# A hybrid streaming-encoder layer: a 32-byte filler in SBUF, later loads of x rows, and a bound on the run ahead at each group's end

## The chip, the cores and the metric

The kernel runs on one core of a Trainium2 chip. The metric is the device time of one execution in microseconds (us), lower is better. The time before is the median of three runs. One further execution was profiled; its trace is what the views of this document are taken from.

## What is computed

One layer on x (256 tokens of 2048 features, float32) and memory (256 tokens), in float32. The reference, cut to what matters here:

```python
h = rms_norm(x, ffn1_norm)
x = x + 0.5 * swiglu_ffn(h, ffn1_w_in, ffn1_w_out)      # 2048 -> 2 x 5632 -> 2048
h = rms_norm(x, mix_norm)
p = h @ w_mix_in                                        # 2048 -> 4096
a_val, a_gate, g_u, g_v = jnp.split(p, split_at, axis=-1)
ya = conv_module_group(a_val, a_gate, ...)              # GLU, causal conv 31, LayerNorm, swish
yb = spatial_gating_group(gelu(g_u), gelu(g_v), ...)    # 8 masked 128x128 mixes
x = x + concat(rms_norm(ya), rms_norm(yb)) @ w_mix_out
h = rms_norm(x, xattn_norm)
x = x + memory_cross_attention(h, rms_norm(mem, mem_norm), w_q, w_kv, w_o)   # 4 heads of 512
h = rms_norm(x, ffn2_norm)
x = x + 0.5 * swiglu_ffn(h, ffn2_w_in, ffn2_w_out)
return rms_norm(x, final_norm)

def swiglu_ffn(h, w_in, w_out):
    gate, up = jnp.split(h @ w_in, 2, axis=-1)
    return (silu(gate) * up) @ w_out
```

Where `rms_norm(x, g)` is x divided by the root of its mean square over the features, times g.

## The kernel before

**Products in two halves.** Every float32 operand is held as a high part (rounded to the matmul's type, "fp32r") and a low part (the rest), and a product is three matmuls: high by high, high by low, low by high. A weight of 128 x 1024 arrives by DMA in a raw place (`raw`, `spare`, `raws_out`), ScalarE (ACT) casts it to the high part (line 451 in the feed-forwards, 128 elsewhere), VectorE (DVE) subtracts to get the low part (lines 428 and 129), and TensorE (PE) uses it as the moving operand, 512 columns at a time, with a 128 x 128 block of x (`x_hl`) or of the hidden layer (`hA`, `hB`, `hC`, `hl_s`) as the stationary one.

**The two feed-forwards** (class `FeedForward`) are the stages the change touches. Each has 11 groups of 512 gate and 512 up columns (`w_in`), then two blocks of 1024 output columns (`w_out`). Group 0 (`begin`) takes 16 weights one after the other, each used by 12 matmuls (`by_two`, lines 358 to 361). Each later group (`group`) takes 8 pairs of weights, some by a scheme with seven products in place of eight (`seven`: four items, of 6, 6, 6 and 3 matmuls, lines 345 to 347), the others plainly (`plain`: two items of 12). Three plain weights of most groups are "summed": their low part is made by two passes of ACT (lines 566, 567) and a DMA that adds, into `hl_s` or `more`, and they need no place of their own. At a group's end its eight PSUM banks are joined by DVE (`joins_eights`, line 702), and `give` makes silu(gate) times up: ACT line 712, DVE line 714, a transpose at line 717.

**What sets the order.** The class `Line` writes the order out by hand: it walks over the items (weights) in order of use. For each it issues the matmuls, then `produce` makes as many later items as it may (cast, and the subtraction of the item made before), then the item's `post` parts follow (joins, `give`, squares, turns). `produce` stops where no place is free, where a load is missing, or at `line.most(used)`, a bound on the number of items made. Before, `most` was `3 + s + max(0, s - 12)` in the first feed-forward (line 1034) and `4 + s + s // 4` in the second (line 1633): both bind in group 0 alone, later the 8 or 9 places bind. Instructions of one engine run in the order in which they were written.

**The start.** `items[k].loads` gives what SP issues beside each weight of group 0: two columns of x (`xT`, line 920), and beside weights 2, 4, 6, 8 half of the rows of x (512 KB, line 889), which ACT squares in place for the RMS norm (line 894) after weights 2, 4, 6, 8. The sum, the root and its refinement (`inverse_root_parts`) follow after items 10 to 12, and the table of silu is loaded after item 13.

**Places in SBUF.** Pools are stacked in the order in which they are opened: `const`, `big` (x_hl, ring, spare, hA, hB and the like), `wraw`, `whl` (`hl`), `ev`, `st` (small tiles), then x's place (`xt`: `gx`, `more`, `raws_out`, `xT`), then the pools of each stage (`own`: `hl_s`, `h`, `z`/`hl_out`, `sums`; `low`: `hl_l`, later `hC`; and in the middle stages `mix` and `attn`). `high` (`hl_h`) is stacked from the other end. A tile `to_64` of 32 bytes in `st` already shifts what follows.

Of the kernel before, what the change touches and what calls it, by code (L numbers as in the profile page):

```python
# [11 lines left out]
F32 = mybir.dt.float32  # L12
# [5 lines left out]
P = 128  # L18
# [20 lines left out]

SUMMED = tuple([()] + [(7, 13)] + [(2, 7, 13)] * 8 + [(2, 7)] for _ in range(2))  # L40

OUT_S = ((9, 11, 13, 15, 17, 19), (9, 11, 13, 15, 17, 19))
# [25 lines left out]
def cuts(n, most):  # L70

    parts = -(-n // most)
    at, out = 0, []
    for i in range(parts):
        size = n // parts + (i < n % parts)
        out.append((at, size))
        at += size
    return out
# [3 lines left out]
def layer(ctx: ExitStack, tc: tile.TileContext, a: dict):  # L82
# [8 lines left out]
    st = ctx.enter_context(tc.tile_pool(name="st", bufs=1))  # L91
# [90 lines left out]
    def ahead(ws, x_hl, per=0.0, accs=None, ks=None, joint=False, end=True, between=None):  # L182

        started = accs is not None and accs[0] is not None
        if not started:
            accs = [ps.tile([P, 2, 256], F32, name="acc") for _ in ws]
        ks = ks or cuts(ws[0].shape[1], 8)
        for i, (k0, kk) in enumerate(ks):
            for at, (w, acc) in enumerate(zip(ws, accs)):
                turn = (i * len(ws) + at) % 2 == 1  # L190
                product_part(acc, w, k0, kk, x_hl, per, i == 0 and not started, end and i == len(ks) - 1, joint, turn)
                if between and i > 0:
                    between.pop(0)()
        return accs
# [45 lines left out]
    def col(name, k):  # L240
        return pv[:, PV[name][0] + k:PV[name][0] + k + 1]
# [125 lines left out]
    def token_accs():  # L367
        return [[bank(ps, "acc") for _ in range(2)] for _ in range(2)]
# [122 lines left out]
    class FeedForward:  # L491
# [6 lines left out]
        def __init__(self, stack, tags, name, x_hl, gain, w_in, w_out, patterns, sums, steps, out_s):  # L498
# [38 lines left out]
            self.line.places.extend(self.in_ring + self.in_low + self.in_high)  # L537
            self.line.raws.extend([Place(lambda: wraw.tile([P, 1024], F32, name="raw")) for _ in range(4)] + self.in_spare)

        def fixed(self, tiles):  # L540
            return [Place(lambda x=x: x) for x in tiles]

# [210 lines left out]
        def begin(self, before, after, scales):  # L753
            acc = []

            def use(k):
                def go(w):
                    if k == 0:
                        acc.extend(token_accs())
                    first = [(t, g) for t in range(2) for g in range(2)] if k == 0 else []  # L760
                    by_two(acc, self.x_hl[:, k], w[:, 0], w[:, 1], k, first, k == KD - 1)
                return go

            items = []
            for k in range(KD):
                held = {}
                items.append(Item(
                    use(k), [(0, self.w_in[0, :, k], None)], held, src=lambda held=held: held[0][0], frees=(0,),
                    post=after.get(k, []),
                ))  # L770
                items[-1].pre = lambda k=k: before(k)
            for i in range(len(self.spairs)):
                for q, part in enumerate(self.sides(i)):
                    items[3 * i + q + 3].post.append(part)
            self.r, parts = scales
            parts = parts + [
                lambda: nc.scalar.activation(out=st.tile([P, 1], F32, name="warm"), in_=ones[:, 0:1], func=AF.Silu)
            ]
            for i, part in enumerate(parts):
                items[14 - len(parts) + i].post.append(part)  # L780
            items[13].post.append(lambda: self.summed_load(self.early))
            items[15].post += [
                lambda: self.give(0, [acc[t][0] for t in range(2)], [acc[t][1] for t in range(2)]),
                lambda: self.summed(self.early),
            ]
            self.ends = [KD]
            return items
# [56 lines left out]
    r_x = st.tile([P, 2], F32, name="r_x2")  # L844
    tot = st.tile([P, 2, 2], F32, name="x_tot")

    def both(*parts):
        return lambda: [part() for part in parts]
# [31 lines left out]
    with ExitStack() as stack:  # L880
        ff = FeedForward(
            stack, ("S1", "S0", "S2"), "a", x_hl, lambda k: gains[:, k:k + 1], a["ffn1_w_in"], a["ffn1_w_out"],
            PATTERNS[0], SUMMED[0], OUT_STEPS[0], OUT_S[0],
        )
        line = ff.line
        squares = [x for y in ff.whole for x in (y[:, 0], y[:, 1])]

        def x_load(c):
            return lambda: nc.sync.dma_start(
                out=squares[c], in_=a["x"][c // 2 * P:(c // 2 + 1) * P, c % 2 * 1024:(c % 2 + 1) * 1024]  # L890
            )

        def x_squares(c):
            return lambda: nc.scalar.activation(
                out=squares[c], in_=squares[c], func=AF.Square, accum_out=tot[:, c % 2, c // 2:c // 2 + 1]
            )
# [4 lines left out]
        root = inverse_root_parts(r_x, r_x, 1.0 / D, RMS_EPS)  # L901
        root[0] = both(
            lambda: nc.vector.tensor_tensor(out=r_x, in0=tot[:, 0], in1=tot[:, 1], op=ALU.add), root[0]
        )
        items = ff.begin(x_arrives, {2 * c + 2: [x_squares(c)] for c in range(4)}, (r_x, root))
        halves = [slice(G, 2 * G), slice(0, G)]

        def early_load():
# [8 lines left out]
        for k in range(1, KD):  # L917
            beside_load = []
            if k % 2 == 0:
                beside_load.append(lambda k=k: nc.sync.dma_start(out=xT[:, k:k + 2], in_=a["xT"][:, k:k + 2]))  # L920
            if k in (2, 4, 6, 8):
                beside_load.append(x_load(k // 2 - 1))
            if k == 11:
                beside_load.append(lambda: nc.sync.dma_start(out=pv, in_=a["pv"]))
            items[k].loads = [(0, a["ffn1_w_in"][0, :, k], both(*beside_load))]
# [85 lines left out]
        parts, _, _ = ff.block(0, first_place, first_done)  # L1011
# [6 lines left out]
        parts, _, _ = ff.block(1, second_place, lambda o: None)  # L1018
# [12 lines left out]
                flat.append(memory_squares((i - at - 3) // 2))  # L1031
        items += flat
        line.add(items)
        line.most = lambda s: 3 + s + max(0, s - 12)
        line.run()
        turns = turned(rest["o2"], 1)
        x_hl = rest["x_hl"]
# [397 lines left out]
    with ExitStack() as stack:  # L1435
        ff = FeedForward(
            stack, ("S0", "S1", "S2"), "b", x_hl, lambda k: col("ffn2_norm", k), a["ffn2_w_in"], a["ffn2_w_out"],
            PATTERNS[1], SUMMED[1], OUT_STEPS[1], OUT_S[1],
        )
        line = ff.line  # L1440
# [15 lines left out]
        r_x = st.tile([P, 2], F32, name="r_x2")  # L1456
        x_tot = []

        def x_sums():
# [10 lines left out]
        items = ff.begin(  # L1470
            lambda k: None, after, (r_x, inverse_root_parts(r_x, lambda: x_tot[0][:, 0, 0:2], 1.0 / D, RMS_EPS))
        )
        items[14].post.append(lambda: given(ff))
        groups(ff, items)
        rest = {}
        sums = st.tile([P, 2, 4], F32, name="sums")
        most = [st.tile([P, 1], F32, name=f"f_most{t}") for t in range(2)]

        def quarters(o):
# [103 lines left out]
        parts, _, _ = ff.block(0, first_place, lambda o: None)  # L1583
# [6 lines left out]
        parts, b, _ = ff.block(1, second_place, None)  # L1590
# [39 lines left out]
        kept[-1].post.append(ending)  # L1630
        items += flat
        line.add(items)
        line.most = lambda s: 4 + s + s // 4
        line.run()


# [79 lines left out]
```

## Time and profile before

| | us |
|---|---|
| median of three runs | 2086.14 |
| lowest and highest of them | 2083.84, 2087.06 |
| the profiled execution | 2084.38 |
| its span, first to last instruction | 2082.6 |
| TensorE busy | 2068.9 |
| VectorE busy | 1703.4 |
| ScalarE busy | 1197.7 |

The page names engines PE (matmul), PEld (weight load of TensorE), DVE (VectorE), ACT (ScalarE), POOL (GpSimd) and SP (the queue that issues most DMAs); `L428` is line 428 of the kernel before. A matmul's row reads `acc<-hl,x_hl`: out, then moving and stationary operand. In the timeline the columns are start and duration in us, then engine, line, operation, out<-in, count, and in brackets the idle time before it and what ended it. Stages on the clock: first feed-forward to about 700 us, mixers and attention to about 1398 us, second feed-forward to 2073 us, then the last norm and the stores.

### The profile page before, as it was taken

The numbers are of one execution on the slowest core, as the hardware profiler recorded it, in microseconds if no ns is written. First come the engines' busy times: TensorE is split into PE (matmuls) and PEld (weight loads), VectorE is DVE, ScalarE is ACT, GpSimd is POOL, SyncE is SP. The second block draws the span as 40 slices with busy tenths as digits, with TensorE's granted clock in tenths as the row PEclk, the third lists the DMA queues.
The fourth block names the chain that finished last, engine by engine and source line by source line (L and its number), as shares of the span: only waits on it lengthen the run. The fifth ranks groups of instructions, "written<-read, shape, count | busy, mean of one in ns | idle before, by whom it ended". The sixth has DMA issues, their size and how long they took to land.

```text
span 2082.6 us, 26581 instructions
## 1 busy us (share of the span) xinstructions
PE 2068.9 (99%) x9544; PEld 1713.2 (82%) x9544; DVE 1703.4 (82%) x2358; ACT 1197.7 (58%) x1514; POOL 62.8 (3%) x81
## 2 busy tenths in 40 slices
PE   9999999999999999999999999999999999999998
PEld 7788888888888888888888899888888888888886
DVE  7998888878987789989887666788888888789875
ACT  7666556646555654444665455566565556565454
POOL 0000000000000000000000000000000000000002
PEclk9999999999999999999999999999999999999999
DMA  8888777869656576656555543678788778797574
GB/s 337 282 249 274 255 232 237 270 181 296 204 197 237 196 238 200 190 178 186 175 192 199 185 160 119 201 296 274 235 254 272 241 225 254 217 260 246 175 215 166
DMA packets 139525, 468.57 MB, mean 225 GB/s; under 512 B 15488, under 2 KB 27136, under 8 KB 138752
## 3 DMA queue, kind: packets, MB, share of 16 engines
q1 hardware_dynamic: 130464, 434.35, 61.2%
q0 software_dynamic: 8352, 31.46, 8.0%
q8 instruction: 75, 1.23, 0.2%
q10 hardware_dynamic: 576, 1.06, 0.1%
q14 instruction: 58, 0.48, 0.1%
HBM read 451.08 MB, written 15.73 MB: 224 GB/s over the span
## 4 chain that ended last, share of the span: by engine, by line
PE 93%; DVE 2%; DMA 1%; ACT 1%; issue 0%; POOL 0%; DVEq 0%; ACTq 0%; SPq 0%
PE acc L359 15%; PE acc L358 15%; PE acc L361 15%; PE acc L158 8%; PE acc L208 5%; PE acc L209 5%; PE acc L207 5%; PE acc L345 5%; PE acc L346 5%; PE acc L347 5%; PE acc L166 4%; PE aux L345 2%; PE aux L346 2%; PE aux L347 2%; DMA raw<-in_memT 1%; DVE hl L129 0%
## 5 line engine op out<-in xcount | busy, mean ns | idle before, releaser
L128 ACT CAST hl<-raw 128x1024 fp32r<-128x1024 f32 (+1 forms) x228 | 235.6, 1035 | 224.6 <-PE acc L209 92.8
L129 DVE TENSOR_TENSOR hl<-raw,hl 128x1024 fp32r<-128x1024 f32 (+1 forms) x228 | 273.9, 1203 | 95.6 <-ACT hl L128 94.5
L451 ACT CAST hl<-raw 128x1024 fp32r<-128x1024 f32 (+1 forms) x136 | 134.3, 1000 | 94.6 <-PE acc L361 38.1
L428 DVE TENSOR_TENSOR hl<-raw,hl 128x1024 fp32r<-128x1024 f32 (+1 forms) x136 | 156.6, 1156 | 26.8 <-ACT hl L451 25.1
L208 PE MATMUL acc<-hl,x_hl 128*128 128x512 f32 x256 | 100.7, 393 | 0.2 <-DVE hl L129 0.2
L208 PE MATMUL acc<-hl,m_hl 128*128 128x512 f32 x256 | 100.3, 392 | 0.0
L209 PE MATMUL acc<-hl,m_hl 128*128 128x512 f32 x256 | 100.3, 392 | 0.0
L209 PE MATMUL acc<-hl,x_hl 128*128 128x512 f32 x256 | 99.9, 390 | 0.0
L359 PE MATMUL acc<-hl,x_hl 128*128 128x512 f32 x248 | 97.0, 391 | 2.6 <-DVE hl L428 2.6
L358 PE MATMUL acc<-hl,x_hl 128*128 128x512 f32 x248 | 97.1, 392 | 0.0
L207 PE MATMUL acc<-hl,m_hl 128*128 128x512 f32 x256 | 90.9, 392 | 0.0
L207 PE MATMUL acc<-hl,x_hl 128*128 128x512 f32 x256 | 90.3, 392 | 0.0
L361 PE MATMUL acc<-hl,x_hl 128*128 128x512 f32 x248 | 76.4, 389 | 0.0
L451 ACT CAST hl<-raws_out 128x1024 fp32r<-128x1024 f32 (+1 forms) x53 | 51.0, 968 | 43.9 <-PE acc L361 22.3
L451 ACT CAST hl<-spare 128x1024 fp32r<-128x1024 f32 (+1 forms) x52 | 49.4, 968 | 34.9 <-DVE spare L635 18.0
L428 DVE TENSOR_TENSOR hl<-raws_out,hl 128x1024 fp32r<-128x1024 f32 (+1 forms) x53 | 59.1, 1121 | 10.5 <-ACT hl L451 9.3
L428 DVE TENSOR_TENSOR hl<-spare,hl 128x1024 fp32r<-128x1024 f32 (+1 forms) x52 | 57.4, 1116 | 12.1 <-ACT hl L451 11.4
L451 ACT CAST hl<-sums 128x1024 fp32r<-128x1024 f32 x34 | 35.7, 1049 | 54.4 <-DVE sums L629 53.8
L359 PE MATMUL acc<-hl_l,x_hl 128*128 128x512 f32 x168 | 66.5, 396 | 0.0
L359 PE MATMUL acc<-more,x_hl 128*128 128x512 f32 x168 | 66.5, 396 | 0.0
L358 PE MATMUL acc<-more,x_hl 128*128 128x512 f32 x168 | 66.5, 396 | 0.0
L358 PE MATMUL acc<-hl_l,x_hl 128*128 128x512 f32 x168 | 66.4, 395 | 0.0
(608 smaller groups left out, 5933.1 us busy)
## 6 DMA issues: line engine op xcount, KB each, us to landing
spare<-in_ffn_w_in SPq DMA_DIRECT2D x200, 512.0 KB, 6.4
raw<-in_ffn_w_in SPq DMA_DIRECT2D x151, 512.0 KB, 6.5
raw<-in_ffn_w_out SPq DMA_DIRECT2D x96, 512.0 KB, 4.4
raws_out<-in_ffn_w_out SPq DMA_DIRECT2D x76, 512.0 KB, 4.9
raw<-in_w_mix_vg SPq DMA_DIRECT2D x32, 512.0 KB, 4.4
raw<-in_w_k SPq DMA_DIRECT2D x32, 512.0 KB, 3.6
raw<-in_w_v SPq DMA_DIRECT2D x32, 512.0 KB, 4.1
raw<-in_w_mix_out SPq DMA_DIRECT2D x32, 512.0 KB, 4.3
```

Source lines behind the costliest of these rows:

```text
L128: nc.scalar.copy(out=hl[:, 0, :size], in_=raw[:, :size])
L129: newest[0] = nc.vector.tensor_tensor(out=hl[:, 1, :size], in0=raw[:, :size], in1=hl[:, 0, :size].bitcast(F32), op=ALU.subtract)
L158: done = nc.tensor.matmul(acc, lhsT=hi[:, k], rhs=xs[k], start=first and k == 0, stop=last and k == kk - 1, skip_group_check=True,)
L207: nc.tensor.matmul(acc[t], lhsT=x[:, 0, s], rhs=hi[:, k], start=k0 + k == 0, stop=False)
L208: nc.tensor.matmul(acc[t], lhsT=x[:, 0, s], rhs=lo[:, k], start=False, stop=False)
L209: nc.tensor.matmul(acc[t], lhsT=x[:, 1, s], rhs=hi[:, k], start=False, stop=k0 + k == nk - 1)
L345: nc.tensor.matmul(acc, lhsT=x[0], rhs=hi, start=first, stop=False)
L358: nc.tensor.matmul(acc[t][g], lhsT=x[:, 0, s], rhs=hi[:, cols[g]], start=(t, g) in first, stop=False)
L359: nc.tensor.matmul(acc[t][g], lhsT=x[:, 0, s], rhs=lo[:, cols[g]], start=False, stop=False)
L361: done = nc.tensor.matmul(acc[t][g], lhsT=x[:, 1, s], rhs=hi[:, cols[g]], start=False, stop=last)
L428: nc.vector.tensor_tensor(out=hl[:, 1, :n], in0=item.raw[:, :n], in1=hl[:, 0, :n].bitcast(F32), op=ALU.subtract)
L451: nc.scalar.copy(out=item.hl[:, 0, :item.n], in_=item.raw[:, :item.n])
```

## The change

Four edits:

- A second tile of 32 bytes (`to_64_too`) in the pool `st`. It is made in the second feed-forward's part of the program, but the pool has one size, so everything behind `st` moves by 32 bytes for the whole program.
- The x rows are loaded beside weights 4, 6, 8, 10 in place of 2, 4, 6, 8, and squared after items 6, 8, 10, 11 in place of 2, 4, 6, 8. Sum, root and refinement come after items 12 to 14, the table of silu after item 15, in both feed-forwards.
- `most` becomes a table. Up to a group's end at item `end`, no more than `end + more[j]` items are made, with `more` 4 for group 0, 6 for group 1, 7 for groups 2 to 9 and 9 for group 10; in group 0 also no more than `s + 4`, or `s + 6` in the second feed-forward. In the two blocks nothing but the places binds.
- The squares of the memory tokens (`memory_squares`) have no edit in the diff.

```diff
+AHEAD = tuple((h, [e, 6, 7, 7, 7, 7, 7, 7, 7, 7, 9]) for h, e in ((4, 4), (6, 4)))
...
+        def ahead(self, rules):
+
+            head, more = rules
+
+            def most(s):
+                for j, end in enumerate(self.ends):
+                    if s <= end:
+                        return min(end + more[j], s + head if j == 0 else 1 << 30)
+                return 1 << 30
+            return most
...
             for i, part in enumerate(parts):
-                items[14 - len(parts) + i].post.append(part)
+                items[16 - len(parts) + i].post.append(part)
...
-        items = ff.begin(x_arrives, {2 * c + 2: [x_squares(c)] for c in range(4)}, (r_x, root))
+        items = ff.begin(x_arrives, {(6, 8, 10, 11)[c]: [x_squares(c)] for c in range(4)}, (r_x, root))
...
-            if k in (2, 4, 6, 8):
-                beside_load.append(x_load(k // 2 - 1))
+            if k in (4, 6, 8, 10):
+                beside_load.append(x_load(k // 2 - 2))
...
-        line.most = lambda s: 3 + s + max(0, s - 12)
+        line.most = ff.ahead(AHEAD[0])
...
         sums = st.tile([P, 2, 4], F32, name="sums")
+        st.tile([P, 8], F32, name="to_64_too")
...
-        line.most = lambda s: 4 + s + s // 4
+        line.most = ff.ahead(AHEAD[1])
```

The places of the built programs, in bytes of a partition:

| tile | place before | modulo 512 | place after | modulo 512 |
|---|---|---|---|---|
| `x_hl`, `ring`, `hA`, `hB` (pool `big`) | 3,584 or 36,352 | 0 | the same | 0 |
| `more_out`, `spare` (pool `big`) | 69,120 | 0 | the same | 0 |
| `hl` (three) | 118,272 to 134,656 | 0 | the same | 0 |
| x's place: `gx`, `more`, `raws_out`, `xT` | 158,176 | 480 | 158,208 | 0 |
| `hl_s` | 175,072 | 480 | 175,104 | 0 |
| `h`, `z`/`hl_out` | 183,264, 191,456 | 480 | 183,296, 191,488 | 0 |
| `hl_l` (two), `hC` | 203,744, 211,936 | 480 | 203,776, 211,968 | 0 |
| `hl_h` | 221,152 | 480 | the same | 480 |

Blocks of a tile that the program reads lie at multiples of 512 bytes from its start.

TensorE's and GpSimd's instructions stand in the same order in both programs. In the changed file the same statements stand 3 to 15 lines lower (428 is 431, 702 is 716).

SP's queue at the start of the program; line 420 loads weights (`raw`, `spare`), 920 columns of x (`gx`), 889 rows of x (`h`, `z`). Before:

```order
L910 DMA raw<-in_ffn_w_in 128x512 x2
L420 DMA raw<-in_ffn_w_in 128x1024
L920 DMA gx<-in_xT 128x512
L889 DMA h<-in_x 128x1024
L420 DMA raw<-in_ffn_w_in 128x1024 x2
L920 DMA gx<-in_xT 128x512
```

After:

```order
L924 DMA raw<-in_ffn_w_in 128x512 x2
L423 DMA raw<-in_ffn_w_in 128x1024
L934 DMA gx<-in_xT 128x512
L423 DMA raw<-in_ffn_w_in 128x1024 x2
L934 DMA gx<-in_xT 128x512
L903 DMA h<-in_x 128x1024
```

The first half of x's rows stands behind weights 2 and 3 and the next columns of x, no longer ahead of them.

DVE at the end of group 1 of the first feed-forward: line 428 subtracts a weight, 628 to 635 make sums of weights, 702 is the join of four banks, 714 the product, 717 the transpose. Before:

```order
L428 TENSOR_TENSOR hl_l_134<-spare,hl_l_134 128x512
L628 TENSOR_TENSOR sums<-raw 128x512
L629 TENSOR_TENSOR sums<-raw 128x512
L428 TENSOR_TENSOR hl_l_135<-raw,hl_l_135 128x1024
L632 TENSOR_TENSOR raw<-sums,raw 128x512
L428 TENSOR_TENSOR more<-sums,more 128x1024
L428 TENSOR_TENSOR hl_h<-raw,hl_h 128x1024
L635 TENSOR_TENSOR raw<-raw 128x512
L428 TENSOR_TENSOR hl<-raw,hl 128x1024
L702 TENSOR_TENSOR spare<-spare,acc 128x512 x4
L714 SCALAR_TENSOR_TENSOR h<-spare,r_x_111,h 128x4x128 x2
L717 STREAM_TRANSPOSE h<-h 128x1024
```

After:

```order
L431 TENSOR_TENSOR hl_l_134<-spare,hl_l_134 128x512
L716 TENSOR_TENSOR spare<-spare,acc 128x512 x4
L728 SCALAR_TENSOR_TENSOR h<-spare,r_x_111,h 128x4x128 x2
L731 STREAM_TRANSPOSE h<-h 128x1024
L642 TENSOR_TENSOR sums<-raw 128x512
L643 TENSOR_TENSOR sums<-raw 128x512
L431 TENSOR_TENSOR hl_l_135<-raw,hl_l_135 128x1024
L646 TENSOR_TENSOR raw<-sums,raw 128x512
L431 TENSOR_TENSOR more<-sums,more 128x1024
L431 TENSOR_TENSOR hl_h<-raw,hl_h 128x1024
```

The group's joins, products and transpose moved ahead of the sums and subtractions for the next group.

ACT at the end of group 0 of the first feed-forward: line 451 casts a weight, 777 loads the table of silu, 712 is silu of the gates, 566 and 567 make a summed weight. Before:

```order
L777 ACT_TABLE_LOAD
L777 ACTIVATE warm<-ones 128x1
L451 CAST ring<-raw 128x512
L451 CAST ring<-raw 128x1024
L451 CAST hl_l_134<-raw 128x1024
L451 CAST hl_l_135<-sums 128x1024
L712 ACTIVATE h<-acc,r_x_111 128x4x128 x2
L566 ACTIVATE hl_s<-spare 128x1024
L567 CAST hl_s<-spare 128x1024
L451 CAST more<-spare 128x1024
```

After:

```order
L454 CAST ring<-raw 128x512
L791 ACT_TABLE_LOAD
L791 ACTIVATE warm<-ones 128x1
L726 ACTIVATE h<-acc,r_x_111 128x4x128 x2
L580 ACTIVATE hl_s<-spare 128x1024
L581 CAST hl_s<-spare 128x1024
L454 CAST ring<-raw 128x1024
L454 CAST hl_l_134<-raw 128x1024
L454 CAST hl_l_135<-sums 128x1024
L454 CAST more<-spare 128x1024
```

Silu and the summed weight moved ahead of three casts.

## The prediction

> **What bounds the kernel now.** I read the page's first part, then the chain of work that ended last, then the windows of the four stages (start, first feed-forward, middle, second feed-forward), and last the list of what TensorE waited for.
>
> ```profile
> PE 2068.9 (99%) x9544; PEld 1713.2 (82%) x9544; DVE 1703.4 (82%) x2358; ACT 1197.7 (58%) x1514; POOL 62.8 (3%) x81
> PE 93%; DVE 2%; DMA 1%; ACT 1%; issue 0%; POOL 0%; DVEq 0%; ACTq 0%; SPq 0%
> 5.77:52.00 46.23, 43.60 (x188) 35.14 (x188) 36.02 (x61) 35.93 (x56) 0.00 (x0) 1.00 0.92 351
> 52.00:700.00 648.00, 647.54 (x2816) 527.09 (x2815) 547.71 (x669) 384.47 (x449) 25.65 (x30) 1.00 0.76 242
> 700.00:1398.00 698.00, 697.81 (x3593) 596.30 (x3592) 558.88 (x943) 380.32 (x552) 1.18 (x9) 1.00 0.58 192
> 1398.00:2073.00 675.00, 675.00 (x2933) 549.91 (x2931) 556.48 (x676) 391.23 (x448) 32.70 (x34) 1.00 0.74 234
> PE acc L359 <- DVE hl L428: 2.6, 2, 1.4
> PE acc L345 <- ACT h L712: 0.4, 1, 0.4
> ```
>
> The columns of a window are its length, then busy time of PE, PEld, DVE, ACT and POOL, then the granted clock, DMA share and GB/s; of a wait us in total, times, longest. TensorE (PE) is busy all through, at clock 1.00. In the two feed-forwards it lacks 2.63 us before 52 us (46.23 - 43.60), 0.46 us up to 700 us, and nothing after 1398 us. So waits can give some 3 us at most. Anything larger must come from how fast matmuls follow one another. Do they all go at one pace? The grouped lines say no (behind the count: busy us, mean ns of one, idle us before):
>
> ```profile
> L359 PE MATMUL acc<-hl_l,x_hl 128*128 128x512 f32 x168 | 66.5, 396 | 0.0
> L359 PE MATMUL acc<-ring,x_hl 128*128 128x512 f32 x152 | 59.2, 390 | 0.0
> L359 PE MATMUL acc<-hl,hl_s 128*128 128x512 f32 x48 | 19.0, 396 | 0.0
> L359 PE MATMUL acc<-hl_h,x_hl 128*128 128x512 f32 x80 | 31.6, 395 | 0.0
> L359 PE MATMUL acc<-hl_h,hl_s 128*128 128x512 f32 x8 | 3.1, 390 | 0.0
> ```
>
> These are one operation of one shape; only the places of the two operands differ. The ends of matmuls are modelled, so I trust their starts more. In the timeline of TensorE, a weight is 12 matmuls:
>
> ```profile
> 1412.81 0.40 PE L358 MATMUL acc<-hl_h,x_hl 128*128 128x512 f32 x1
> ...
> 1415.61 0.39 PE L345 MATMUL acc<-hl,ring 128*128 128x512 f32 x1
> ...
> 1420.40 0.39 PE L358 MATMUL acc<-ring,x_hl 128*128 128x512 f32 x1
> ...
> 1423.12 0.40 PE L358 MATMUL acc<-hl_l,x_hl 128*128 128x512 f32 x1
> ...
> 1425.92 0.40 PE L345 MATMUL acc<-hl_l,ring 128*128 128x512 f32 x1
> ```
>
> Twelve matmuls from `ring` take 1423.12 - 1420.40 = 2.72 us (226.7 ns each); twelve from `hl_l` take 1425.92 - 1423.12 = 2.80 us (233.3 ns), twelve from `hl_h` 2.80 us too. The table of places in the section on the change tells them apart: `ring`, `hl`, `x_hl` begin at 0 modulo 512, `hl_l`, `hl_h`, `hl_s` at 480. Is it the place itself, or that moving and stationary operand differ? The six matmuls with both at 480 answer:
>
> ```profile
> 477.99 0.39 PE L358 MATMUL acc<-hl_h,hl_s 128*128 128x512 f32 x1
> ...
> 479.35 0.40 PE L358 MATMUL acc<-hl,hl_s 128*128 128x512 f32 x1
> ```
>
> They take 1.36 us, 226.7 ns each: the fast pace, out of the same `hl_h` that is slow beside `x_hl`. I read it so: **a matmul whose two operands begin at different offsets costs 6.65 ns more** (233.3 - 226.7).
>
> **The change part by part.**
>
> *The filler.* It moves x's place and all that is stacked behind it from 480 to 0; `hl_h`, which hangs from the top, stays at 480. TensorE's order is the same in both programs, so only the counts matter. These are TensorE's matmuls by tile, over the span, for `hl_l`, `more`, `hl_s`, `hC`, `hl_out`, `hl_h` in turn:
>
> ```profile
> 0.00:2082.60 2082.60, 189.41 (x774) 1.00 0.70 225
> 0.00:2082.60 2082.60, 159.86 (x642) 1.00 0.70 225
> 0.00:2082.60 2082.60, 128.62 (x528) 1.00 0.70 225
> 0.00:2082.60 2082.60, 84.45 (x354) 1.00 0.70 225
> 0.00:2082.60 2082.60, 76.05 (x300) 1.00 0.70 225
> 0.00:2082.60 2082.60, 140.71 (x558) 1.00 0.70 225
> ```
>
> The first five make 2598. Out of these go pairs that agree already: `hl_h` with `hl_s` 24 and with `hC` 24 (in the grouped lines three lines of 8 each), and `hl_out` with `hC` 54 (three of 12, three of 6), which stands in two rows, so 108 off. That leaves 2442 pairs that agree afterwards and do not now. The 48 pairs of `hl_h` with `hl_s` or `hC` go the other way: 2442 - 48 = 2394 net. 2394 x 6.65 ns = **-15.9 us**. By the group means (396 against 390) it would be 2394 x 6 = 14.4 us, the lower end. At the upper end I add 2 us: after each slow item some matmuls of the next are still late (the six before 477.99 took 1.38 us, 0.02 more than the six after), for up to 100 such passages, since slow items come in runs. What makes it worth its full sum is that nothing else fills the time: DVE, the next busiest, is at 547.71 of 648 us and 556.48 of 675; with 8 us less in each stage that is 86% and 83%.
>
> Two rules of the Trainium skill speak against this term. "SBUF — State Buffer", Specifications (TRN2), gives lines of 16 bytes, and 480 is a multiple of 16, so a start at 480 would cost nothing; "TensorE: Matmul & The Clock Gate", Step-by-step, has the moving operand and the weight load on two independent read ports, so that one could not slow the other. By both, this term would be 0; the 1.36 us for six of one pair against 2.80 us for twelve of the other do not agree with them, since shape and granted clock are the same.
>
> *The x rows two weights later.* SP issues each row half, 512 KB, behind two more weights. The second wait of TensorE comes from there:
>
> ```profile
> 2.60 0.47 SPq L889 DMA_DIRECT2D h<-in_x  x1
> 11.84 1.05 ACT L451 CAST hl<-raw 128x1024 fp32r<-128x1024 f32 x1 [2.94 <-DMA raw<-in_ffn_w_in]
> 13.73 1.22 DVE L428 TENSOR_TENSOR hl<-raw,hl 128x1024 fp32r<-128x1024 f32 x1
> 10.61 0.50 PE L359 MATMUL acc<-hl,x_hl 128*128 128x512 f32 x1 [1.24 <-DVE hl L428]
> 15.01 0.50 PE L359 MATMUL acc<-hl,x_hl 128*128 128x512 f32 x1 [1.39 <-DVE hl L428]
> ```
>
> ACT waited 2.94 us for weight 2, which landed at 11.84 us behind the row issued at 2.60. At the 351 GB/s of the start's window 512 KB take 1.5 us; without them weight 2 lands near 10.3, its subtraction on DVE ends about 13.4 instead of 14.95, and TensorE asks for it at 13.62 (15.01 - 1.39). So the second wait goes: **-1.4 us**. The first wait, for weight 1, hangs on the x columns issued before the row: it may stay, or go in part (0 to -1.2). The squares, two to four weights later, are hidden: ACT is busy 35.93 of 46.23 us. The four loads later are free as long as the rows land before group 0 ends, 40 us on. In the second feed-forward, which shares this code, only the reciprocal root moves, by two weights; nothing needs it until group 0 ends.
>
> *The bound on the run ahead.* It adds no instruction. At a group's end DVE's joins now stand before three or four subtractions instead of behind them. A gain needs TensorE to wait for joins now: 0.4 us, once, behind `h L712`. A loss needs a weight to be late. Rows of a group end (the next group's first matmul is at 1584.21):
>
> ```profile
> 1584.21 0.40 PE L345 MATMUL acc<-hl_l,ring 128*128 128x512 f32 x1
> 1582.82 1.22 DVE L428 TENSOR_TENSOR ring<-raw,ring 128x1024 fp32r<-128x1024 f32 x1 [2.73 <-ACT ring L451]
> 1583.96 2.47 DVE L702 TENSOR_TENSOR spare<-spare,acc 128x512 f32<-128x512 f32 x4
> 1586.35 1.41 DVE L714 SCALAR_TENSOR_TENSOR h<-spare,r_x,h 128x512 f32<-128x512 f32 x2
> 1587.79 1.25 DVE L717 STREAM_TRANSPOSE h<-h 128x1024 f32<-128x1024 f32 x1
> ```
>
> Joins, products and transpose take 5.1 us of DVE, then 0.6 for a sum of half a weight (four joins of that size take 2.47) and 1.22 for the first subtraction behind them: 6.9 us. Six items lie ready, 45 matmuls or 10.2 us: 3.3 us to spare.
>
> At the end of group 0 only four items may be made, and the fifth, a plain weight, is due 21 matmuls or 4.8 us after the next group's first. ACT now has this ahead of its cast:
>
> ```profile
> 56.03 1.25 ACT L712 ACTIVATE h<-acc,r_x 128x512 f32<-128x512 f32 x2
> 57.18 1.06 ACT L566 ACTIVATE hl_s<-spare 128x1024 fp32r<-128x1024 f32 x1
> 58.13 1.05 ACT L567 CAST hl_s<-spare 128x1024 fp32r<-128x1024 f32 x1
> ```
>
> The second pass of `h` can end about 0.65 us after that first matmul (half of 1.25), the summed weight takes 2.0, the cast 1.05, the subtraction 1.22: 4.9 us, 0.1 to 0.2 late, in each feed-forward. Against it the wait of 0.4 behind `h L712` goes, since `h` no longer stands behind a cast. I take **0** net, and keep -1 to +2.
>
> *Sum.* -15.9 - 1.4 = -17.3. The profiled execution took 2084.38 us (span 2082.6 and 1.8 around it): 2067.1. The median of the runs is 1.76 us above that execution: 2086.14 - 17.3 = **2068.8 us**.
>
> **The rivals.**
>
> *The place, not the difference.* All tiles at 480 lie above byte 158,000 of a partition, all others below. If matmuls are slow for a pair that spans the two regions, whatever the offset, the filler gives nothing: -1.4 alone leaves 2084.7. For it: the trace has no upper tile at 0 and no lower one at 480. Against it: it must call a pair within the upper region fast (1.36 us for six), so it needs two regions that disturb each other only when both are read, which is odder than two offsets. The two rules of the skill named above, taken at their word, would end here too. I give it 9%.
>
> *Half.* The difference acts through a finer pattern than the one offset seen, and some pairs stay slow: half of 15.9 and 1.4, 2076.8. Against it stand the lower tiles, all at 0 with each other and all at the fast pace. 4%.
>
> *Starved after the joins.* The bound trades the joins' delay for a delay of weights. DVE's 5.1 us at each of 20 group ends also hold back the loads that wait for its subtractions. It decides once a weight is more than the 3.3 us late that six ready items leave; a full 5.1 us of lateness would cost 1.8 us at each end, 36 us in all: 2086.1 - 17.3 + 36 = 2104.8. For it: DVE is busy 85% already. Against it: DVE now idles before the joins instead (2.7 us before its last subtraction there), so little of the work is truly later. 3%.
>
> *It doesn't do what it says.* "Memory's squares later": no edit moves the squares of the memory tokens, and their place in ACT's order is the same; it would be x's squares that are meant. The price is 0 either way.
>
> **How the numbers follow.** My forecast has 84%. Its own range is from 2086.1 - 15.9 - 2 - 2.6 - 1 = 2064.6 to 2086.1 - 14.4 + 2 = 2073.7; with the spread of the runs before (2083.84 to 2087.06) I take 2063.5 to 2077, which holds nearly all of the forecast's chance and "half": 8 in 10 and a little over. 0.2% (4.2 us) is about what a measurement of this kernel can tell from no change. Faster by more: forecast and half, 88%. Within: the place rival, 9%. Slower: 3%.
>
> **What would show it.** In the changed profile `hl_l`, `more`, `hl_s` beside `x_hl` should stand at 389 or 390 ns and twelve of them in 2.72 us, `hl_h` beside `x_hl` still at 395, and `hl_h` beside `hl_s`, fast now, should turn slow. The second wait near 15 us should be gone. TensorE's idle time between groups should stay under a microsecond in all. The prediction is wrong if `hl_l` keeps 396, or if DVE or a weight's DMA shows as a releaser of TensorE at group starts.

## The result, and the profile after

| | before | after |
|---|---|---|
| median of four runs, us | 2086.19 | 2067.57 |
| lowest and highest, us | 2083.84, 2087.06 | 2066.76, 2069.33 |
| the profiled execution, us | 2084.38 | 2067.29 |
| its span, us | 2082.6 | 2065.5 |

After stands to before as 0.9914, with a 95% interval of 0.9896 to 0.9931: 18.6 us are gone, 17.3 were forecast. The total is right. The experiments show that the largest of its three terms was right, that the gain of the rows did not last, and that the zero of the bound hides waits on both sides that were larger than thought.

From the page of the changed kernel, busy time of each engine:

```profile
PE 2052.6 (99%) x9544; PEld 1714.4 (83%) x9544; DVE 1704.0 (82%) x2358; ACT 1194.0 (58%) x1514; POOL 62.7 (3%) x81
```

Its windows (length; busy time and count of PE, PEld, DVE, ACT, POOL; granted clock, DMA share, GB/s), and then its list of waits (us in total, times, longest):

```profile
5.77:52.00 46.23, 43.96 (x186) 35.53 (x185) 35.18 (x60) 34.09 (x53) 0.00 (x0) 0.96 0.95 362
52.00:700.00 648.00, 648.00 (x2856) 534.46 (x2855) 551.59 (x672) 389.43 (x458) 25.64 (x30) 1.00 0.77 243
1382.00:2056.00 674.00, 674.00 (x2964) 555.87 (x2962) 565.20 (x690) 392.65 (x454) 32.69 (x34) 1.00 0.75 239
```

```profile
PE acc L362 <- DVE hl L431: 2.3, 1, 2.3
```

TensorE was the bound and still is. In the same 648 us, busy without a gap, it starts 2856 matmuls in place of 2816: 226.9 ns each instead of 230.1. That is the filler at work. The last row is the surprise: the two waits of 1.24 and 1.39 us at the start have become one of 2.3 us, not one of 1.2.

The grouped lines of the changed kernel (count, busy us, mean ns) show which tiles changed pace:

```profile
L362 PE MATMUL acc<-hl_l,x_hl 128*128 128x512 f32 x168 | 65.4, 389 | 0.0
L362 PE MATMUL acc<-more,x_hl 128*128 128x512 f32 x168 | 65.4, 390 | 0.0
L361 PE MATMUL acc<-hl,hl_s 128*128 128x512 f32 x48 | 18.7, 389 | 0.0
L362 PE MATMUL acc<-hl_h,x_hl 128*128 128x512 f32 x80 | 31.7, 396 | 0.0
```

And its timeline of TensorE in the second feed-forward, first row of each run of one tile:

```profile
1398.37 0.39 PE L361 MATMUL acc<-hl_l,x_hl 128*128 128x512 f32 x1
...
1403.81 0.40 PE L361 MATMUL acc<-hl_h,x_hl 128*128 128x512 f32 x1
...
1406.62 0.39 PE L348 MATMUL acc<-hl,ring 128*128 128x512 f32 x1
```

Two weights of `hl_l`, 24 matmuls, take 5.44 us, 226.7 ns each, where twelve took 2.80 before. The twelve of `hl_h`, which did not move, still take 2.81. The row of `hl_h` at 1403.81 is the one that stood at 1412.81 before: 9.0 us are gained by then.

The start and group 1, first two rows of the kernel before, then the timeline of the changed kernel and one window of its start:

```profile
17.63 0.39 PE L358 MATMUL acc<-ring,x_hl 128*128 128x512 f32 x1
...
59.42 0.39 PE L358 MATMUL acc<-ring,x_hl 128*128 128x512 f32 x1
```

```profile
8.78 0.39 PE L361 MATMUL acc<-hl,x_hl 128*128 128x512 f32 x1
...
11.43 0.50 PE L362 MATMUL acc<-hl,x_hl 128*128 128x512 f32 x1 [2.27 <-DVE hl L431]
...
13.32 0.63 PE L362 MATMUL acc<-hl,x_hl 128*128 128x512 f32 x1
...
13.75 0.63 PE L361 MATMUL acc<-hl,x_hl 128*128 128x512 f32 x1
...
18.40 0.39 PE L361 MATMUL acc<-ring,x_hl 128*128 128x512 f32 x1
...
59.40 0.40 PE L361 MATMUL acc<-ring,x_hl 128*128 128x512 f32 x1
```

```profile
12.40:15.90 3.50, 3.50 (x10) 2.69 (x10) 2.80 (x4) 1.25 (x3) 0.00 (x0) 0.51 1.03 404
```

Behind the 2.27 us the matmuls stand 0.43 us apart (13.32, 13.75), and the granted clock is 0.51 for some 3.4 us. So the first matmul from `ring`, at 17.63 us before, comes at 18.40, 0.8 us later than before, although less time is spent waiting. Yet in group 1 the changed kernel is level: its matmul at 59.40 started at 59.42 before. Something between 18 and 59 us evens out the start, and what it is became the main question.

### The profile page after: what moved, and what is told of

It reads as the page before. It is cut to its first block, busy times and chain, and to the rows that moved or that the text cites. A ratio compares the mean times of both kernels' runs of the same rounds, so it can differ in the third digit from the quotient of the medians.

```text
span 2065.5 us, 26562 instructions
## 1 busy us (share of the span) xinstructions
PE 2052.6 (99%) x9544; PEld 1714.4 (83%) x9544; DVE 1704.0 (82%) x2358; ACT 1194.0 (58%) x1514; POOL 62.7 (3%) x81
## 4 chain that ended last, share of the span: by engine, by line
PE 96%; DVE 2%; DMA 1%; ACT 1%; issue 0%; POOL 0%; SPq 0%; DVEq 0%; ACTq 0%
PE acc L362 16%; PE acc L361 16%; PE acc L364 16%; PE acc L161 9%; PE acc L211 5%; PE acc L212 5%; PE acc L210 5%; PE acc L348 5%; PE acc L349 5%; PE acc L350 5%; PE acc L169 4%; PE aux L349 2%; PE aux L348 2%; PE aux L350 2%; DVE hl L132 0%; DMA raw<-in_w_mix_vg 0%
## 5 line engine op out<-in xcount | busy, mean ns | idle before, releaser
L716 DVE TENSOR_TENSOR spare<-spare,acc 128x512 f32<-128x512 f32 x80 | 51.2, 684 | 48.1 <-PE acc L364 46.7
L454 ACT CAST hl<-spare 128x1024 fp32r<-128x1024 f32 (+1 forms) x52 | 48.9, 967 | 32.2 <-DVE spare L649 17.9
```

The source lines that it names most:

```text
L454: nc.scalar.copy(out=item.hl[:, 0, :item.n], in_=item.raw[:, :item.n])
```

## The experiments

Each run is compared with runs of the kernel before on the same chip. "Start" is the first matmul from `ring`; "group 1" is the third matmul of the first plain weight of group 1 (its fifth item), at 59.40 us above. A start is called quick where the first matmul from `ring` comes between 15.5 and 16.2 us.

**The filler by itself, and the change without it.**

```diff
+        st.tile([P, 8], F32, name="to_64_too")      # filler_alone: added to the kernel before
-        st.tile([P, 8], F32, name="to_64_too")      # no_filler: taken from the changed kernel
```

> The kernel before with the 32-byte filler and nothing else. Theory (the filler carries the gain by the pace of matmuls; the x rows' move cost 0.8 us at the start, the bound gave 0.4): between the first and the last matmul 17.6 us go, so 2086.2 - 17.6 = 2068.6 us; the two waits of 1.24 and 1.39 us near 10.6 and 15.0 us stay, the wait of 0.4 us behind h stays, and the granted clock stays 1.00 up to 20 us. Rival (the prediction's sum: filler 15.9, x rows 1.4): 2070.3 us. Rival (the other two edits carry several us): 2072 us or more.

> The changed kernel without its filler: x rows later and the bound alone. Theory: 2086.2 + 0.8 (start) - 0.4 (wait behind h) = 2086.6 us, with all tiles of x's place at 396 ns again. Rival (the prediction: x rows give 1.4, the bound 0): 2084.8 us.

`filler_alone`: 2071.2 us (2068.77 to 2072.77), ratio 0.9924 (0.991 to 0.9937). `no_filler`: 2085.04 us (2083.47 to 2094.33), ratio 0.9993 (0.9982 to 1.0004). The filler carries the gain, and the other two edits without it come to nothing that can be measured. On the same chip the kernel before took 2087.03 us, so the filler by itself is worth 15.8 us: the 15.9 of the prediction, and 1.8 less than the 17.6 that this run's own forecast took from the first comparison. `no_filler` lies between its two forecasts and decides for neither. The list of waits of `filler_alone` says where some of the 17.6 went:

```profile
PE acc L359 <- DVE hl L428: 2.5, 2, 1.4
PE acc L345 <- ACT h L712: 1.0, 1, 1.0
PE acc L345 <- DVE spare L702: 0.8, 1, 0.8
```

The wait behind `h`, forecast to stay at 0.4, has grown, and none was listed for a join before. A faster TensorE reaches the ends of groups 0 and 1 earlier and waits there for what ACT and DVE have not done.

**The x rows back, the bound back.**

```diff
-        items = ff.begin(x_arrives, {(6, 8, 10, 11)[c]: [x_squares(c)] for c in range(4)}, (r_x, root))
+        items = ff.begin(x_arrives, {2 * c + 2: [x_squares(c)] for c in range(4)}, (r_x, root))
-            if k in (4, 6, 8, 10):
-                beside_load.append(x_load(k // 2 - 2))
+            if k in (2, 4, 6, 8):
+                beside_load.append(x_load(k // 2 - 1))
-                items[16 - len(parts) + i].post.append(part)
+                items[14 - len(parts) + i].post.append(part)
```

The above is `rows_back`; `bound_back` is this alone:

```diff
-        line.most = ff.ahead(AHEAD[0])
+        line.most = lambda s: 3 + s + max(0, s - 12)
-        line.most = ff.ahead(AHEAD[1])
+        line.most = lambda s: 4 + s + s // 4
```

> The changed kernel with x's rows (and their squares and root) where they were before. Theory: TensorE waits twice, 1.2 and 1.4 us, near 10.6 and 15.0 us instead of once for 2.3; no stretch at granted clock 0.5 behind them; the third weight's first matmul stands 0.8 us earlier than in the changed kernel: 2067.6 - 0.8 = 2066.8 us. Rival (the move of the rows gives the 1.4 us predicted, the half clock is due to something else and stays): 2069.0 us, with matmuls 427 ns apart between 12 and 16 us again.

> The changed kernel with the old limits of the run ahead. Theory: the wait of 0.4 us behind h at the end of group 0 comes back and nothing else: 2067.6 + 0.4 = 2068.0 us. Rival (the bound is worth several us, by joins that no longer stand behind subtractions): 2070 us or more, with waits at group ends. Rival (the bound costs time through late weights): under 2066.5 us.

`rows_back`: 2067.09 us (2065.74 to 2067.62), ratio 0.99 (0.9887 to 0.9914). The total fits, the reason given does not: there is one wait again, and half clock behind it, from 11.7 to 15.0 us:

```profile
11.32 0.50 PE L362 MATMUL acc<-hl,x_hl 128*128 128x512 f32 x1 [1.81 <-DVE hl L431]
```

So half clock does not belong to the later rows.

`bound_back`: 2069.35 us (2068.39 to 2070.02), ratio 0.9912 (0.9898 to 0.9925), by its total not to be told from the changed kernel. Its timeline of ACT and then of TensorE at the end of group 0 says more:

```profile
53.56 1.05 ACT L454 CAST hl_l<-sums 128x1024 fp32r<-128x1024 f32 x1 [1.96 <-DVE sums L643]
54.63 1.28 ACT L791 ACT_TABLE_LOAD   x1
55.92 0.20 ACT L791 ACTIVATE warm<-ones 128x1 f32<-128x1 f32 x1
56.03 1.25 ACT L726 ACTIVATE h<-acc,r_x 128x512 f32<-128x512 f32 x2
56.75 0.50 PE L348 MATMUL acc<-hl,x_hl 128*128 128x512 f32 x1 [2.65 <-ACT h L726]
...
59.38 0.39 PE L361 MATMUL acc<-ring,x_hl 128*128 128x512 f32 x1
```

In this run the start was quick: one wait of 1.26 us, no half clock. All of that is gone at 59.38 us. Without the bound, ACT casts a weight of group 1 ahead of `h`, and that weight is a sum that DVE has not made yet; ACT stands idle 1.96 us, `h` is late, and TensorE waits 2.65 us for its banks. At the end of group 1 it waits another 0.95 us for a join. With the bound no trace lists a wait for that join. The wait behind `h` is gone from both traces of the changed kernel, though 0.5 us of it are left in `no_filler` and 1.0 in `all_32`. The prediction put this side at the 0.4 us that the kernel before lost there, but the loss grows as TensorE comes earlier.

**The changed kernel once more.** No edit.

> The changed kernel once more, unedited, as the measure for the runs beside it and for what varies at its start. Theory (how long TensorE stands idle for the second weight is decided by when the DMAs land in that run, 1.1 to 2.3 us; only over some 1.5 us does half clock follow; and what is won or lost there is evened out by the end of group 0, since the first four items of group 1 are held by ACT and DVE): 2067.6 us, and with an idle time near 1.1 us and no half clock the 280th matmul record would still start at 69.0 to 69.5 us. Rival (half clock belongs to the changed order): idle 2.3 us and matmuls 427 ns apart again.

2068.43 us (2066.81 to 2071.13), ratio 0.9919 (0.9903 to 0.9936). Its timeline of TensorE:

```profile
10.30 0.50 PE L362 MATMUL acc<-hl,x_hl 128*128 128x512 f32 x1 [1.14 <-DVE hl L431]
...
15.67 0.39 PE L361 MATMUL acc<-ring,x_hl 128*128 128x512 f32 x1
...
57.26 0.50 PE L349 MATMUL acc<-ring,x_hl 128*128 128x512 f32 x1 [1.42 <-DVE ring L431]
...
58.62 0.51 PE L362 MATMUL acc<-ring,x_hl 128*128 128x512 f32 x1 [0.40 <-DVE ring L431]
58.97 0.40 PE L361 MATMUL acc<-ring,x_hl 128*128 128x512 f32 x1
```

The same program, 2.7 us quicker at the start (15.67 against 18.40, and 2.0 ahead of the kernel before), is 0.4 us quicker in group 1 (58.97 against 59.40). Most of the 2.3 us between them go to the two waits, 1.8 us of idle time: 1.42 us for the low part of the fourth item of group 1, 0.40 us for that of the fifth. The traces of `no_filler`, `all_32`, `places_a` and `high_0`, whose start is as quick, list the same two waits of 1.4 and 0.4 us. What holds the fourth item stands in DVE's order, first in `after_2`, then in the kernel before:

```profile
55.39 1.25 DVE L731 STREAM_TRANSPOSE h<-h 128x1024 f32<-128x1024 f32 x1
56.55 2.01 DVE L431 TENSOR_TENSOR ring<-raw,ring 128x512 fp32r<-128x512 f32 x2
```

```profile
51.62 0.68 DVE L428 TENSOR_TENSOR ring<-raw,ring 128x512 fp32r<-128x512 f32 x1
```

At the end of group 0 four items may be made ahead, and an item is subtracted when the next one is made. So the bound puts the subtraction of the fourth behind the products and the transpose of `h`; before, it stood ahead of them. The prediction looked at the fifth item alone and expected it 0.1 to 0.2 us late, with an `h` that ACT ends 0.65 us after group 1's first matmul. In the profiled execution of the result, after its slow start, `h` ends 1.0 us after that matmul, and the fifth item is 0.1 us late, as expected. In `after_2` `h` ends 3.3 us after it (54.49 against 51.22): TensorE came earlier, `h` hardly did.

That the profiled executions of the result are level in group 1 has other reasons than these waits: of the 0.8 us that the changed kernel is late at 18 us, 0.3 are won back in group 0 by its faster pairs, and 0.6 where the kernel before waits behind `h` and the changed one does not.

**Does the difference of the two places cost, or the place?** `all_32` shifts everything but `hl_h` to 32 modulo 512; `places_a` spreads the tiles; `high_0` moves `hl_h` to 0.

```diff
+    const.tile([P, 8], F32, name="shift")            # all_32: ahead of pool big
...
+    xt.tile([P, 8], F32, name="at_x")                # places_a: x's place at 32
+            self.own.tile([P, 8], F32, name="at_s")  # hl_s, hl_out, hC at 64
+            low.tile([P, 16], F32, name="at_a")      # hl_a at 128
+            low.tile([P, 80], F32, name="at_b")      # hl_b at 448
+            high.tile([P, 56], F32, name="at_h")     # hl_h at 256
...
             highs = [high.tile([P, 2, 1024], F32R, name="hl_h")]
+            high.tile([P, 120], F32, name="to_0")    # high_0
```

> The changed kernel with one more filler of 32 bytes ahead of all tiles below x's place: every operand but hl_h begins at 32 modulo 512, none at 0. Theory (the difference of the two operands' offsets is what costs): 7836 pairs still agree, the pace stays 227 ns, 2067.6 us. Rival (a start at 0 modulo 512 is what a matmul needs): 7836 pairs turn slow, 7836 x 6.65 ns = 52 us, 2120 us. Rival (it is the region above 158,000 bytes that an operand must reach aligned): the pairs of lower tiles stay at 227 ns and the upper ones go to 233 ns, 2084 us.

> The changed kernel with fillers that put x's place at 32, hl_s and hl_out and hC at 64, the two hl_l (here named hl_a and hl_b) at 128 and 448, hl_h at 256 modulo 512; the lower tiles stay at 0. Theory (any difference costs the same 6.65 ns): 3000 slow pairs instead of 558, 2067.6 + 2442 x 6.65 ns = 2083.8 us, and more, hl_s, hl_a, hl_b, hl_h beside x_hl all at 233 ns from start to start. Rival (only 64-byte lines count, so a difference of 64, 128, 256 or 448 is free): only the 642 pairs with x's place slow, 2067.6 + 0.6 = 2068.2 us. Rival (the cost grows with the difference): different paces by tile.

> The changed kernel with a filler of 480 bytes behind hl_h, which moves it from 480 to 0: all 8394 pairs agree. Theory: the last 558 slow pairs turn fast, 558 x 6.65 ns = 3.7 us, 2067.6 - 3.7 = 2063.9 us, spread over both feed-forwards. Rival (in the changed kernel something other than matmuls bounds these stretches): no change, 2067.6 us.

`all_32`: 2069.87 us (2066.7 to 2073.24), ratio 0.9922 (0.9906 to 0.9938). Its grouped lines:

```profile
L363 PE MATMUL acc<-hl_l,x_hl 128*128 128x512 f32 x168 | 65.4, 389 | 0.0
L363 PE MATMUL acc<-hl_h,x_hl 128*128 128x512 f32 x80 | 31.5, 394 | 0.0
```

No operand begins at 0 modulo 512 and the pace is the fast one; `hl_h`, at 480 beside 32, is slow. So it is the difference, and both "a start at 0" and "the upper region" fall.

`places_a`: 2080.07 us (2079.16 to 2081.01), ratio 0.9971 (0.996 to 0.9983): 11.6 us above `after_2`, where 16.2 were forecast for "any difference costs the same". Its grouped lines:

```profile
L362 PE MATMUL acc<-more,x_hl 128*128 128x512 f32 x168 | 66.4, 395 | 0.0
L362 PE MATMUL acc<-hl_a,x_hl 128*128 128x512 f32 x88 | 35.0, 397 | 0.0
L362 PE MATMUL acc<-hl_b,x_hl 128*128 128x512 f32 x80 | 31.5, 394 | 0.0
L362 PE MATMUL acc<-hl,hC 128*128 128x512 f32 x60 | 23.8, 397 | 0.0
L362 PE MATMUL acc<-hl_h,hA 128*128 128x512 f32 x24 | 9.3, 389 | 0.0
```

Differences of 32 (`more`), 128 (`hl_a`), 448 (`hl_b`) and of 64 with the stationary operand ahead (`hl` beside `hC`) are slow; 256 (`hl_h` beside `hA`) is free. From start to start within one pair of tiles, averaged over the trace:

```
moving, stationary   offsets modulo 512   pairs   mean ns
more, x_hl            32,  0               506     233.2
hl, hl_s               0, 64               132     233.5
hl_s, x_hl            64,  0               308     229.8
hl_a, x_hl           128,  0               282     232.6
hl_b, x_hl           448,  0               256     232.6
hl_h, hA             256,  0                66     226.6
hl_h, x_hl           256,  0               260     229.6
```

A moving operand 64 bytes ahead costs half or more (`hl_out` beside `hA` and `hB`: 230.8 and 231.8). `hl_h` at 256 beside `x_hl` looks mixed, because slow weights often stand ahead of it. The starts in the same trace separate the two effects: with eight or more fast matmuls ahead of it, `hl_h` stands at 227.2 ns beside `x_hl` (80 pairs) and 226.7 beside `hA` and `more_out` (120); among the first six behind a slow pair it stands at 230.7 beside `x_hl`, no slower than pairs that agree stand there (231.6). So 256 costs nothing of its own, while 192 (`hl_h` beside `hl_s` and `hC`, 232.4 and 233.4) is slow. What has to agree is thus nearer to the place modulo 256 than modulo 512, with the small differences not all alike. Lines of 64 bytes as the only thing that counts are ruled out by 128 and 448.

`high_0`: 2061.82 us (2061.48 to 2062.08), ratio 0.9883 (0.9868 to 0.9898). All pairs agree, and `hl_h` stands at 389 ns. The gain over `after_2` is 6.6 us by the medians and 4.7 by the two profiled executions (2062.08 against 2066.81), against 3.7 forecast. The forecast left out what slow pairs do to the matmuls behind them: by the starts in the changed kernel's trace the 558 slow pairs cost 3.9 us and the matmuls right behind them 1.4 more. These 5.3 cover the 4.7; the rest of the 6.6 is within the spread of `after_2`, whose runs lie 4.3 us apart.

**Why the start is evened out.** `root_back` puts the squares and the root back two weights and leaves the rows' loads late:

```diff
-        items = ff.begin(x_arrives, {(6, 8, 10, 11)[c]: [x_squares(c)] for c in range(4)}, (r_x, root))
+        items = ff.begin(x_arrives, {2 * c + 2: [x_squares(c)] for c in range(4)}, (r_x, root))
-                items[16 - len(parts) + i].post.append(part)
+                items[14 - len(parts) + i].post.append(part)
```

> The changed kernel with the squares of x's rows and the reciprocal root two weights earlier again, as before the change; the rows' loads stay two weights later. Theory (what is won at the start is lost at the end of group 0, because ACT's two table loads of 1.28 us for the root now stand right ahead of h, so that the fifth item of group 1 comes 1.4 + 0.4 us late): h starts 1 to 1.5 us earlier, the waits behind ring near 57 to 59 us fall from 1.8 us to under 0.7, the first matmul after them starts near 58.5 instead of 59.66 us, total 2068.0 - 1.2 = 2066.8 us. Rival (the order ahead of h doesn't matter, DMA or DVE sets group 1's start): the two waits stay at 1.8 us and the total at 2068 us.

2065.26 us (2064.14 to 2066.05), ratio 0.9893 (0.9877 to 0.9908). ACT ahead of `h`, first in `after_2`, then in `root_back` with TensorE's wait:

```profile
51.83 1.28 ACT L791 ACT_TABLE_LOAD   x1
53.13 0.20 ACT L791 ACTIVATE warm<-ones 128x1 f32<-128x1 f32 x1
53.24 1.25 ACT L726 ACTIVATE h<-acc,r_x 128x512 f32<-128x512 f32 x2
```

```profile
48.70 1.28 ACT L791 ACT_TABLE_LOAD   x1
...
51.56 1.26 ACT L726 ACTIVATE h<-acc,r_x 128x512 f32<-128x512 f32 x2
...
56.96 0.50 PE L362 MATMUL acc<-ring,x_hl 128*128 128x512 f32 x1 [0.38 <-DVE ring L431]
57.30 0.39 PE L361 MATMUL acc<-ring,x_hl 128*128 128x512 f32 x1
```

With the table of silu loaded two weights earlier, `h` starts 1.7 us earlier, and 1.4 of these are the load and the first use of that table. The wait for the fourth item is gone, the other is 0.38 us, and group 1 stands at 57.30 instead of 58.97. The two totals alone don't settle it, since their intervals overlap. The waits do: 1.4 and 0.4 us in all five traces with a quick start, the later root and the bound, 0.4 alone in `root_back` and `best` (0.6 and 0.4 in `best_5`, below). The theory holds in this form: the load of the silu table, which moved with the root, and not DMA, took back most of what the later rows gave. What the later squares add wasn't separated.

**A version faster than the changed kernel.** `best` joins `root_back` and `high_0`, and at the start has DVE subtract a weight ahead of the next weight's columns of x; `best_5` was meant to allow a fifth item ahead of `h`.

```diff
         def x_arrives(k):
+            if line.ahead is not None:
+                line.subtract()
             gained(x_hl, k, xT[:, k], gains[:, k:k + 1])
...
-AHEAD = tuple((h, [e, 6, 7, 7, 7, 7, 7, 7, 7, 7, 9]) for h, e in ((4, 4), (6, 4)))
+AHEAD = tuple((h, [e, 6, 7, 7, 7, 7, 7, 7, 7, 7, 9]) for h, e in ((4, 5), (6, 4)))
```

> The kernel of root_back with hl_h at 0 (as in high_0), and with each weight's subtraction on DVE ahead of the next weight's x columns at the start. Theory: 2061.8 (high_0) - 1.2 (root) and the wait for the second weight, 1.1 to 2.3 us before, at 0.3 us or less with another of about 1 us behind the third; some of it is lost again at group 1's start: 2060 us. Rival (start and group 1 even out whatever is done): 2061.8 us.

> The kernel best with five items instead of four allowed ahead of h at the end of group 0. Theory: the fifth item is ready, but h waits for one more cast of 1.05 us on ACT and the wait moves from ring to h: within 1 us of best. Rival (the bound of four is one too few once the root is out of the way): 1 us or more faster than best.

`best`: 2059.33 us (2058.25 to 2060.41), ratio 0.9866 (0.9848 to 0.9885). `best_5`: 2060.09 us (2058.62 to 2063.27), ratio 0.987 (0.9853 to 0.9888). `best_5` tests nothing about the bound: `most` takes the smaller of `end + 5` and `s + 4`, which at `s = end = 16` is 20 as before, and in the two traces the instructions of TensorE, ACT and DVE stand in the same order from first to last. It is `best` once more, and whether a fifth item would help stays open. The whole list of what TensorE waits for in `best` (the first row is the start of the program):

```profile
PE aux L239 <- DVE ones L236: 1.1, 1, 1.1
PE acc L362 <- DVE ring L431: 0.4, 1, 0.4
```

The wait for the second weight is gone, and the wait of about 1 us that had been expected behind the third did not appear. What remains of the time is TensorE's own pace.

## Why the prediction was right, point by point

- *What bounds the kernel.* Right: in the two feed-forwards the time followed the pace of matmuls.
- *The filler, -15.9 us (14.4 to 17.9).* Right in mechanism, and in size but for one part. From group 1, where both profiled kernels are level (59.42 and 59.40), to the end 17.1 us go: 9.0 up to the `hl_h` row of the second feed-forward, 8.1 behind it. The starts in the two traces account for all of it. The slow pairs, 2952 before and 558 after, cost 19.8 and 3.9 us beyond 226.7 ns each: 15.9 less. The first six matmuls behind a slow pair start 230.1 ns apart before and 230.3 after, though their own operands agree; there are 133 such passages before and 66 after, 2.58 and 1.44 us: another 1.14 less. This is the addition for change-overs that the prediction put at the upper end only, at up to 2 us. `hl_h` beside `hl_s` turned slow (396 ns), as was said.
- *The rows, -1.4 us.* Wrong as a gain that lasts. Without half clock the start gained 2.0 us (`after_2`), with it lost 0.8, and neither reached group 1 in full. The step that failed is "the squares, two to four weights later, are hidden: ACT is busy 35.93 of 46.23 us", and with it the root that "nothing needs until group 0 ends". A share of 78% over 46 us said nothing of the last 3 us, where the table of silu, moved together with the root, stands right ahead of `h`.
- *The bound, 0 (-1 to +2).* Both sides exist, their sizes were worked out at the moment that TensorE had before. With an earlier TensorE, the waits without the bound are 2.65 + 0.95 us (`bound_back`). With it the fourth and the fifth item cost 1.42 + 0.40 us (`after_2`), where the sum had the fifth alone. In the total the bound's worth stays within the spread of the runs.
- *The signs.* The second wait is gone and the paces are as named. But one sign of being wrong, DVE as a releaser of TensorE at group starts, shows in `after_2` (1.42 and 0.40 us in group 1), and the idle time there is above the microsecond that was allowed. The profiled execution of the result doesn't show it; there half clock had made TensorE 2.7 us later at the start.
- *Why the sum held.* In the profiled executions the rows gave about 1.4 us less than forecast, the filler about 1.2 more. That two small misses cancel is luck; the forecast was good because its one large term was. By the runs, whose interval spans 14 to 22 us, neither miss could be seen.
- *The rivals.* "The place, not the difference" fell with the upper tiles at 0 and with `all_32`. "Half" fell as well, though a finer pattern exists (`places_a`): it does not show at the offsets that the change meets. "Starved" came about in small at one group end only: 1.8 us for late weights in group 1 of `after_2`, where the rival had 1.8 us at each of 20 ends. That the memory's squares don't move held.

## What to carry to other kernels

When a group of identical matmuls shows two durations, compare where the two operands begin before looking at queues; here a filler of 32 bytes was worth 0.8%, and aligning the last odd tile some 5 us more. A gain ahead of a meeting point (here `h` at the end of group 0) is worth only what the latest of the other engines leaves, so price it at that point, with the engine's order just ahead of it, and not by the share of its busy time. A wait that is small now is no measure of what an edit there is worth once another edit makes the waiting engine faster.

## What the runs showed of the hardware that was not expected

- *The two operands of a matmul.* With 512 columns of 32-bit data, operands whose places differ by 32, 128 or 448 bytes modulo 512 took 232.6 to 233.2 ns from start to start in place of 226.7 (`places_a`), those that differ by 480 took 233.4 (the kernel before), and 64 with the stationary operand ahead 233.5; 256 beside `hA` took 226.6. Why the difference costs isn't shown.
- *Behind a slow pair.* In the kernel before, the first six matmuls behind a slow pair start 230.1 ns apart on average, although their own operands agree; further on it is 226.8.
- *Half clock at the start.* Behind an idle time of 2.27 us (the changed kernel) and 1.81 us (`rows_back`) matmuls stood 427 ns apart at a granted clock of 0.51 for 3.4 us. Behind 1.46 us or less at the same place the clock stayed at 1.00, and in `bound_back` even behind 2.65 us at the end of group 0. "TensorE: Matmul & The Clock Gate" of the Trainium skill, Part 1, gives a free-running window of about 3.4 us, 426.7 ns at half clock, and half clock after an idle window; length and pace agree, but TensorE was not idle for as long as a whole window here, so less than that can suffice. Which idle time brings half clock stays open.
- *A stretch near the end of the first feed-forward.* In `all_32` and `no_filler` TensorE lost 2 to 3 us between 500 and 540 us, here in `all_32`:

```profile
500.00:530.00 30.00, 27.15 (x114) 20.73 (x113) 22.85 (x41) 15.66 (x25) 0.00 (x0) 1.00 1.00 250
```

In `all_32` the DMA engines are busy all through there (share 1.00), and casts wait for rows that come back from memory. The profiled executions of the other programs lose 0.2 us or less there. It may be part of the spread between runs; its cause is open.
